# Router logits from the residual stream: the norm's scale folded into the router, the token's root and the shift put on the sums, scale and shift on the gathered rows after their turn

## The chip, the cores and the metric

The kernel runs on one core of a Trainium2 chip. The metric is the device time of one execution in microseconds (us). TensorE (PE) multiplies, VectorE (DVE) and ScalarE (ACT) do elementwise work, GpSimd (POOL) issues the gathers, SyncE (SP) issues the other transfers; each engine runs its instructions strictly in order and waits on semaphores for the others.

## The reference, cut to what matters

The model has two layers. The second ends in a mixture of experts: the stream `x` (512 tokens of 1024 numbers) is normed and modulated, a router picks two of eight experts per token, and each expert is a SwiGLU of 3584 hidden numbers over the tokens that chose it.

```python
h = rmsnorm(x, norm2_g) * (1 + sc2) + sh2      # x * root * A + B, root per token, A and B per column
logits = h @ router                            # 1024 x 8
top_logit, top_idx = lax.top_k(logits, 2)
gates = softmax(top_logit)
y = (silu(h[tok] @ w1[e]) * (h[tok] @ w3[e])) @ w2[e] * gate
out = x + g2 * scatter_add(y)
```

The kernel keeps fp32 accuracy by splitting each operand of a product into a high and a low part (fp32r), and multiplying the parts.

## The kernel before, in words

The stages follow each other: a first norm, the RG-LRU mixer, a dense SwiGLU, attention, `route`, `moe`, `final`. Up to `route` the stream lies turned in SBUF: `xT`, partitions are columns of the model (8 blocks of 128, `k`), the free axis is tokens.

`attention` leaves its last output projections to `route`: `self.attn_outs(cs, segs)` does, for column blocks `cs` and a range of tokens, 24 matmuls per block (8 `k` times three products of parts, L155, L157, L159) and adds the result to `xT` (L384). `route` takes the tokens in two halves of 256. It projects blocks 4 to 7 of the first half, then calls `norm` for it (squares L361, their sum L363, root L335 and L336, the root spread over the partitions by PE L344, times scale L372, plus shift L377, split L166 and L167) with block 4 of the second half put between. `norm` writes `h2` (fp32, turned) and the parts for the logits. Blocks 5 to 7 of the second half follow, then its norm; while that runs, the first half's logits are made (L983). `rows` turns 128 tokens back to rows (8 transposes, L973), copies them from PSUM (L975) and writes them to DRAM: `xd` holds the stream's rows, to which the experts later add, and `h2d` the normed rows, from which the experts gather. After the second half's logits come top-2, the counts, the ranks of the experts by load and the places of the tokens (L1023 to L1080), all small DVE work.

`moe` takes the experts in four pairs, a big and a small one. `gather` makes the token indices (L1174 to L1194) and fetches rows of `h2d` by an indirect DMA on POOL (L1190). The weights come as 1 MB tiles `raw` on SP's queue (L1155), four buffers deep; the first needs the expert's number, `eidi` (L1421), in an SP register. Each `raw` is split in two halves: `hi` by ACT (L166), `lo` by DVE (L167). `gathered` turns the gathered rows (L1231, into PSUM pool `tr`, two buffers) and splits them into `XG`, the parts that the expert's first matmuls read; one ACT and one DVE instruction serve four column blocks. `hidden` (128 tokens; L1262 to L1264) and `hidden_t` (more tokens; L1286 to L1289) are woven; so are `outputs` and `outputs_t`. Within the output stage of a pair the next pair is gathered and turned.

The program text is not the order on the engines: a list scheduler orders each engine's instructions when the kernel is built, by dependencies and its own costs.

Of the kernel before, what the change touches and what calls it, by code (L numbers as in the profile page):

```python
# [10 lines left out]
F32 = mybir.dt.float32  # L11
F32R = mybir.dt.float32r
# [3 lines left out]
AF = mybir.ActivationFunctionType  # L16
ALU = mybir.AluOpType
# [68 lines left out]
class Net:  # L86
# [859 lines left out]

    def route(self):

        nc, I, tc = self.nc, self.I, self.tc
        V, S, mm = nc.vector, nc.scalar, nc.tensor.matmul  # L950
        LAT = SEGS[:1]
# [6 lines left out]
        with ExitStack() as st:  # L958
            one = self.pool(st, "rt1", 1)
            two = self.pool(st, "rt2", 2)  # L960
            rraw = one.tile([P, KT, 8], F32, name="rraw")
            nc.gpsimd.dma_start(rraw, I["moe_router"][0].rearrange("(k p) e -> p k e", p=P))
            rt = one.tile([P, KT, 16], F32R, name="rt")
            V.tensor_copy(rt[:, :, 0:8], rraw)
            V.tensor_tensor(rt[:, :, 8:16], rraw, rt[:, :, 0:8].bitcast(F32), op=ALU.subtract)
            h2 = one.tile([P, KT, L], F32, name="h2")
            lg = one.tile([P, 4, 8], F32, name="lg")

            def rows(src, dst, j):

                ps = self.ptile("prow")
                for k in range(KT):
                    nc.tensor.transpose(ps[:, k * P:(k + 1) * P], src[:, k, j * P:(j + 1) * P], self.ident)  # L973
                ht = two.tile([P, D], F32, tag="ht", name="ht", bufs=3)
                S.activation(ht, ps, AF.Copy)  # L975
                nc.sync.dma_start(dst[j * P:(j + 1) * P, :], ht)

            def logits(parts, i):

                pl = self.sp.tile([P, 512], F32, tag="sm", name="plog")  # L980
                for k in range(KT):
                    for x in parts:
                        mm(pl[0:16, 0:C], rt[:, k], x[:, k], start=(k == 0 and x is parts[0]), stop=(k == KT - 1 and x is parts[1]))  # L983
                lrow = two.tile([16, C], F32, tag="lrow", name="lrow")
                V.tensor_copy(lrow, pl[0:16, 0:C])
                pt = self.sp.tile([P, 512], F32, tag="sm", name="plt")
                for j in range(2):
                    nc.tensor.transpose(pt[:, 16 * j:16 * j + 16], lrow[:, j * P:(j + 1) * P], self.ident[:16, :16])
                pv = pt[:, 0:32].rearrange("p (j e) -> p j e", j=2)
                d = lg[:, 2 * i:2 * i + 2]  # L990
                V.tensor_copy(d, pv[:, :, 8:16])
                V.tensor_tensor(d, pv[:, :, 0:8], d, op=ALU.add)

            x = self.xT[0]
            parts = [[self.big.tile([P, KT, C], F32R, tag=f"{x}{1 - i}", name=f"n{x}") for x in ("HH", "HL")] for i in range(2)]
            self.attn_outs(range(4, 8), HALVES[:1])
            self.norm(1, 1, HALVES[0], two, out=parts[0], full=h2, between=lambda: self.attn_outs([4], HALVES[1:]))
            for c in (5, 6, 7):  # L1000
                self.attn_outs([c], HALVES[1:])
                if c < 7:
                    rows(x, self.xd, c - 5)

            def beside():
                logits(parts[0], 0)
                rows(x, self.xd, 2)

            self.norm(1, 1, HALVES[1], two, out=parts[1], full=h2, between=beside)
            for j in range(2):  # L1010
                rows(h2, self.h2d, j)
            rows(x, self.xd, 3)
            logits(parts[1], 1)
            for j in (2, 3):
                rows(h2, self.h2d, j)
            self.dumpx("x3")
            self.wst_stack.close()
            self.keep = kp = self.pool(self.ctx, "keep", 1, side="right")
# [204 lines left out]
    def gathered(self, X):  # L1223

        n = X["n"]
        XG = X["XG"] = self.mo1.tile([P, KT, 2 * n], F32R, tag=f"XG{X['slot']}", name="XG")
        for gx, a, m in X["gxs"]:
            for k0 in (0, 4):
                pt = self.tr.tile([P, 512], F32, tag="tr", name="pgx")
                for k in range(4):  # L1230
                    self.nc.tensor.transpose(pt[:, k * m:(k + 1) * m], gx[:m, (k0 + k) * P:(k0 + k + 1) * P], self.ident[:m, :m])  # L1231
                pv = pt[:, :4 * m].rearrange("p (k t) -> p k t", k=4)
                self.split(XG[:, k0:k0 + 4, a:a + m], XG[:, k0:k0 + 4, n + a:n + a + m], pv)
            yield

    def flush(self):
# [13 lines left out]
    def hidden_512(self, X, ch):  # L1250
        nc = self.nc
        V, S, mm = nc.vector, nc.scalar, nc.tensor.matmul
        xh, xl = X["XG"][:, :, 0:P], X["XG"][:, :, P:2 * P]
        both = self.psum()
# [43 lines left out]
    def hidden_t(self, X):  # L1298
# [247 lines left out]
```

## Time and profile before

| | |
|---|---|
| median of 3 runs | 2392.67 us (2392.31 to 2395.7) |
| profiled execution | 2390.89 us, of which the span from first to last instruction 2389.1 us |
| TensorE's mean granted clock | 0.988 of full speed |
| PE busy | 2310.9 us (97%) |
| DVE, ACT busy | 1731.5 us (72%), 1326.3 us (56%) |
| `route` and the start of `moe` | about 1075 to 1170 us of the span |

The page's line of engine busy time over 40 slices shows PE at 9 tenths or more nearly everywhere; the first slice and the twentieth (about 1135 to 1195 us) have 7 tenths, the last 5. The change lies in and just before that twentieth slice. Times in a timeline are counted from the start of the span.

### The profile page before, as it was taken

How to read it: one execution, taken by the hardware profiler on the slowest of the kernel's cores; microseconds unless marked ns; L12 is line 12 of the kernel's file. 1: busy time of each engine (PE TensorE's matmuls, PEld its weight loads, DVE VectorE, ACT ScalarE, POOL GpSimd, SP SyncE). 2: the span in 40 equal slices, each digit the busy share in tenths (PEclk: the TensorE clock that was granted, in tenths of full speed). 3: DMA queues.
4: the chain of work that ended last, by engine and by line, in shares of the span. 5: the costliest groups of instructions: out<-in, count | busy, mean ns of one | idle time of the engine just before them, and what ended most of it. 6: DMA issues, size and time to landing. Idle time of an engine off the chain costs nothing. (4 is left out here: it accounts for less than half of the span.)

```text
span 2389.1 us, 37939 instructions
## 1 busy us (share of the span) xinstructions
PE 2310.9 (97%) x14911; PEld 2064.7 (86%) x14911; DVE 1731.5 (72%) x2610; ACT 1326.3 (56%) x1882; POOL 44.4 (2%) x40
## 2 busy tenths in 40 slices
PE   7999999999999999999799999999999999999995
PEld 6887888888888888898699999999999999999994
DVE  7668776555564366795888877888778887788874
ACT  5687342112211146774566665767667776677763
POOL 0000000000000000000100000000010000100000
PEclk9999999999999999999799999999999999999997
DMA  9255423243431112001888889999899998999995
GB/s 306 80 168 193 160 71 124 84 145 124 141 124 53 54 45 71 19 2 57 298 286 286 293 279 287 319 302 310 290 309 314 300 311 289 311 322 307 307 314 170
DMA packets 349434, 491.18 MB, mean 206 GB/s; under 512 B 8848, under 2 KB 247696, under 8 KB 349248
## 3 DMA queue, kind: packets, MB, share of 16 engines
q1 hardware_dynamic: 346032, 477.50, 60.3%
q0 software_dynamic: 3216, 11.18, 2.0%
q8 instruction: 119, 1.95, 0.3%
q14 instruction: 67, 0.55, 0.1%
HBM read 477.04 MB, written 11.60 MB: 205 GB/s over the span
## 5 line engine op out<-in xcount | busy, mean ns | idle before, releaser
L167 DVE TENSOR_TENSOR lo<-raw,hi 128x1024 fp32r<-128x1024 f32 (+2 forms) x856 | 930.4, 1107 | 250.5 <-ACT hi L166 245.3
L166 ACT ACTIVATE hi<-raw 128x1024 fp32r<-128x1024 f32 (+2 forms) x856 | 803.8, 964 | 474.2 <-PE hb L1289 228.4
L1289 PE MATMUL hb<-XG,hi 128*128 128x320 f32 (+2 forms) x1568 | 428.8, 348 | 0.0
L1287 PE MATMUL hb<-XG,lo 128*128 128x160 f32 (+2 forms) x1792 | 398.6, 242 | 0.0
L1287 PEld LDWEIGHTS hb<-XG,lo 128*128 128x128 f32 x1792 | 332.1, 190 | 4.4
L1289 PEld LDWEIGHTS hb<-XG,hi 128*128 128x128 f32 x1568 | 295.1, 188 | 0.0
L1289 PE MATMUL hb<-HT,hi 128*128 128x320 f32 (+2 forms) x864 | 231.4, 348 | 0.0
L1287 PE MATMUL hb<-HT,lo 128*128 128x160 f32 (+2 forms) x896 | 211.1, 239 | 0.0
L157 PE MATMUL p<-HL,hi 128*128 128x512 f32 (+1 forms) x704 | 191.3, 338 | 0.0
L159 PE MATMUL p<-HH,lo 128*128 128x512 f32 (+1 forms) x704 | 191.1, 337 | 0.0
L155 PE MATMUL p<-HH,hi 128*128 128x512 f32 (+1 forms) x704 | 191.1, 338 | 0.0
L1262 PE MATMUL hb<-hi,XG 128*128 128x512 f32 x448 | 177.9, 397 | 1.6 <-ACT XG L166 1.6
L1263 PE MATMUL hb<-hi,XG 128*128 128x512 f32 x448 | 177.3, 396 | 0.0
L1264 PE MATMUL hb<-lo,XG 128*128 128x512 f32 x448 | 176.8, 395 | 0.0
L1287 PEld LDWEIGHTS hb<-HT,lo 128*128 128x128 f32 x896 | 169.9, 190 | 2.3
L1289 PEld LDWEIGHTS hb<-HT,hi 128*128 128x128 f32 x864 | 162.2, 188 | 1.6
L653 DVE TENSOR_TENSOR sg<-p,sg 128x768 f32<-128x768 f32 (+2 forms) x26 | 21.7, 835 | 151.3 <-PE p L159 151.3
L1294 ACT ACTIVATE t<-hb 128x320 f32<-128x320 f32 (+2 forms) x128 | 56.9, 445 | 126.2 <-PE hb L1289 126.2
L157 PEld LDWEIGHTS p<-HL,hi 128*128 128x128 f32 x704 | 112.9, 189 | 15.2
L155 PEld LDWEIGHTS p<-HH,hi 128*128 128x128 f32 x704 | 112.8, 189 | 15.3
L159 PEld LDWEIGHTS p<-HH,lo 128*128 128x128 f32 x704 | 112.7, 189 | 15.3
L384 DVE SCALAR_TENSOR_TENSOR xT<-py,acol,xT 128x512 f32<-128x512 f32 (+1 forms) x176 | 101.5, 611 | 22.4 <-PE py L159 21.9
(410 smaller groups left out, 4070.0 us busy)
## 6 DMA issues: line engine op xcount, KB each, us to landing
raw<-in_moe_w_dram SPq DMA_DIRECT2D x280, 1024.0 KB, 5.2
raw<-in_moe_w_dram SPq DMA_DIRECT2D x64, 896.0 KB, 4.9
raw<-in_ffn_w_dram SPq DMA_DIRECT2D x33, 1024.0 KB, 5.2
raw<-in_ada_w_dram SPq DMA_DIRECT2D x24, 1024.0 KB, 7.0
araw<-in_ada_w_dram SPq DMA_DIRECT2D x48, 512.0 KB, 3.7
raw<-in_rg_w_in_dram SPq DMA_DIRECT2D x16, 512.0 KB, 6.6
raw<-in_attn_w_qkv_dram SPq DMA_DIRECT2D x6, 1024.0 KB, 5.0
raw<-in_rg_w_out_dram SPq DMA_DIRECT2D x4, 1024.0 KB, 8.1
```

The costliest lines, as they stand in the source:

```text
L155: mm(ps[:, s:e], wh, xh[v][:, s - v * L:e - v * L], start=(first and i == 0), stop=False)
L157: mm(ps[:, s:e], wh, xl[v][:, s - v * L:e - v * L], start=False, stop=False)
L159: mm(ps[:, s:e], wl, xh[v][:, s - v * L:e - v * L], start=False, stop=(last and i == n - 1))
L166: self.nc.scalar.activation(hi, src, AF.Copy)
L167: self.nc.vector.tensor_tensor(lo, src, hi.bitcast(F32), op=ALU.subtract)
L384: self.nc.vector.scalar_tensor_tensor(x, ps[:, s:e], gate[:, k, v:v + 1], x, op0=ALU.mult, op1=ALU.add)
L1262: mm(ps, xh[:, kk], hi[:, k], start=(kk == 0), stop=False)
L1263: mm(ps, xl[:, kk], hi[:, k], start=False, stop=False)
L1264: mm(ps, xh[:, kk], lo[:, k], start=False, stop=(kk == 7))
L1287: mm(ps[:, 0:n], wl, x[:, 0:n], start=False, stop=False)
L1289: mm(ps[:, 0:2 * n], wh, x, start=False, stop=last)
L1294: self.nc.scalar.activation(t, ps[:, :, n:2 * n], AF.Copy)
```

## The change

Before, the normed stream was computed in full for all 512 tokens, used for the logits, turned to rows and written to `h2d`. Now three factors are taken apart. With A the column scale, B the column shift and r the token's root, the logits are r * (x @ (A * router)) + B @ router. So the router is multiplied by A once (`ra`), `B @ router` is made once (`pb`, `br`), the split parts are those of `x` itself (`split_x`), and `finish` puts r and `br` on the eight sums of a token. The root no longer goes over the partitions; it stays a column, one number per token row. `rows` turns `x` once and copies it twice, once times r for `h2d` and once as it is for `xd`. The rows gathered from `h2d` thus lack A and B; `gathered` puts them on after the turn, where columns are partitions: per column block, one ACT instruction for the high part and one DVE instruction for the fp32 value `z`, then one subtraction for the low part of four blocks.

```diff
+            A, B = self.A[1][:, 1], self.mod(1, 3)
+            ra = one.tile([P, KT, 8], F32, name="ra")
+            V.tensor_tensor(ra, rraw, A[:, :, 0:1].to_broadcast((P, KT, 8)), op=ALU.mult)
...
+            for k in range(KT):
+                mm(pb[:, 0:8], B[:, k, 0:1].to_broadcast((P, P)), rraw[:, k], start=(k == 0), stop=(k == KT - 1))
...
+            def split_x(i, *ks):
+                s, e, _ = HALVES[i]
+                for k in ks:
+                    self.split(parts[i][0][:, k], parts[i][1][:, k], x[:, k, s:e])
...
+            def rows(js, r):
...
+                for dst in (self.h2d, self.xd):
+                    for j, ps in zip(js, pss):
+                        ht = two.tile([P, D], F32, tag="ht", name="ht", bufs=3)
+                        S.activation(ht, ps, AF.Copy, scale=r[:, j % 2:j % 2 + 1] if dst is self.h2d else 1.0)
+                        nc.sync.dma_start(dst[j * P:(j + 1) * P, :], ht)
...
-            self.attn_outs(range(4, 8), HALVES[:1])
-            self.norm(1, 1, HALVES[0], two, out=parts[0], full=h2, between=lambda: self.attn_outs([4], HALVES[1:]))
...
-            self.norm(1, 1, HALVES[1], two, out=parts[1], full=h2, between=beside)
-            for j in range(2):
-                rows(h2, self.h2d, j)
-            rows(x, self.xd, 3)
-            logits(parts[1], 1)
-            for j in (2, 3):
-                rows(h2, self.h2d, j)
+            def finish(i, r):
+                for j in range(2):
+                    d = lg[:, 2 * i + j]
+                    V.scalar_tensor_tensor(d, d, r[:, j:j + 1], br, op0=ALU.mult, op1=ALU.add)
...
+            r0 = inverse(0)
+            logits(0)
+            finish(0, r0)
             for c in (5, 6, 7):
                 self.attn_outs([c], HALVES[1:])
+                split_x(1, c)
                 if c < 7:
-                    rows(x, self.xd, c - 5)
+                    rows((c - 5,), r0)
+            logits(1)
+            r1 = inverse(1)
+            finish(1, r1)
+            rows((2, 3), r1)
...
     def gathered(self, X):
...
-                pv = pt[:, :4 * m].rearrange("p (k t) -> p k t", k=4)
-                self.split(XG[:, k0:k0 + 4, a:a + m], XG[:, k0:k0 + 4, n + a:n + a + m], pv)
+                z = self.mo2.tile([P, 512], F32, tag="sg", name="z")
+                for k in range(4):
+                    c = slice(k * m, (k + 1) * m)
+                    sc, b = A[:, k0 + k, 0:1], B[:, k0 + k, 0:1]
+                    S.activation(XG[:, k0 + k, a:a + m], pt[:, c], AF.Identity, bias=b, scale=sc)
+                    self.nc.vector.tensor_scalar(z[:, c], pt[:, c], sc, b, op0=ALU.mult, op1=ALU.add)
+                zv = z[:, :4 * m].rearrange("p (k t) -> p k t", k=4)
+                hi = XG[:, k0:k0 + 4, a:a + m].bitcast(F32)
+                self.nc.vector.tensor_tensor(XG[:, k0:k0 + 4, n + a:n + a + m], zv, hi, op=ALU.subtract)
```

`inverse(i)` is what `norm` did up to the root: squares on ACT, their sum on DVE, one PE product and the root.

The order on VectorE around the second half's logits, before (`h2` is the normed stream, `nHH` and `nHL` its parts, `lrow` the logits out of PSUM, `lg` the logits turned):

```order
L372 SCALAR_TENSOR_TENSOR h2_9734<-xT0_2118,A1_95,rs_10125 128x256
L167 TENSOR_TENSOR nHL_9739<-h2_9734,nHH_9738 128x256 x2
L1023 MAX mx_10248<-lg_9735 128x8 x2
L1024 MAX_INDEX mi_10249<-mx_10248,lg_9735 128x8 x2
L167 TENSOR_TENSOR nHL_9739<-h2_9734,nHH_9738 128x256 x3
L985 COPY lrow_10213<-plog_10196 16x256
L991 COPY lg_9735<-plt_10215 128x16
L992 TENSOR_TENSOR lg_9735<-plt_10215,lg_9735 128x16
L1023 MAX mx_10248<-lg_9735 128x8 x2
```

and of the changed kernel, from the last addition to the stream (`po1`) on (`xHH`, `xHL` are the parts of the stream, `rcol` the root):

```order
L384 SCALAR_TENSOR_TENSOR xT0_2118<-po1_10073,acol1_93,xT0_2118 128x256
L1118 CAST iota_10255<-ct_75 128x192
L1120 CAST tokid_10257<-ct_75 128x12
L1157 MEMSET cum_10410 128x1
L167 TENSOR_TENSOR xHL_9751<-xT0_2118,xHH_9750 128x256
L994 TENSOR_TENSOR acc_10125<-acc_10125,sq_10145 128x256
L1016 COPY lrow_10118<-plog_10101 16x256
L1022 COPY lg_9747<-plt_10120 128x16
L1023 TENSOR_TENSOR lg_9747<-plt_10120,lg_9747 128x16
L336 RECIPROCAL rcol_10151<-rcol_10151 128x2
L1028 SCALAR_TENSOR_TENSOR lg_9747<-lg_9747,rcol_10151,br_9745 128x8 x2
L1058 MAX mx_10190<-lg_9747 128x8 x2
```

Between the last addition and the logits there is now one split; the eight multiplications by scale and root are gone.

The order on ScalarE at the start of `moe`, before (`XG_10525` is the input of the small expert, the one whose matmuls stand first on PE, `XG_10510` that of the big one; `hi_10561` and `hi_10565` are halves of the first weight tile, `hi_10585` begins the second):

```order
L1150 ACTIVATE g2b_10491<-hb_10492 128x1024
L166 ACTIVATE hi_10561<-raw_10559 128x1024
L166 ACTIVATE XG_10525<-pgx_10526 128x4x128
L166 ACTIVATE XG_10525<-pgx_10533 128x4x128
L166 ACTIVATE hi_10565<-raw_10559 128x1024
L166 ACTIVATE hi_10585<-raw_10583 128x1024
```

and of the changed kernel (`XG_10483` is the small expert's input; `hi_10551`, `hi_10555` are of the first weight tile, `hi_10575`, `hi_10579` of the second, `hi_10621` of the third):

```order
L166 ACTIVATE hi_10555<-raw_10549 128x1024
L1272 ACTIVATE XG_10452<-pgx_10468,acol1_93,A1_95 128x128
L1185 ACTIVATE g2b_10433<-hb_10434 128x1024
L1272 ACTIVATE XG_10483<-pgx_10484,acol1_93,A1_95 128x128
L166 ACTIVATE hi_10575<-raw_10573 128x1024
L166 ACTIVATE hi_10579<-raw_10573 128x1024
L1272 ACTIVATE XG_10452<-pgx_10468,acol1_93,A1_95 128x128
L1272 ACTIVATE XG_10483<-pgx_10484,acol1_93,A1_95 128x128
L166 ACTIVATE hi_10621<-raw_10619 128x1024
L1272 ACTIVATE XG_10483<-pgx_10499,acol1_93,A1_95 128x128
L1272 ACTIVATE XG_10483<-pgx_10484,acol1_93,A1_95 128x128
```

The small expert's input now stands behind the splits of three weight tiles, where it stood behind one half of the first.

The order on VectorE there, before (`lo` belongs to `hi`; `room` is a scratch table):

```order
L167 TENSOR_TENSOR lo_10562<-raw_10559,hi_10561 128x1024
L1140 TENSOR_TENSOR room_10457<-eid_10301,room_10457 128x128
L167 TENSOR_TENSOR XG_10525<-pgx_10526,XG_10525 128x4x128
L1141 TENSOR_REDUCE room_10457<-room_10457 128x16
L167 TENSOR_TENSOR XG_10525<-pgx_10533,XG_10525 128x4x128
```

and of the changed kernel the end of the same stretch, which begins at `lo_10552`, 26 instructions ahead of the last row here:

```order
L1273 TENSOR_SCALAR z_10504<-pgx_10499,A1_95,acol1_93 128x128
L1176 TENSOR_REDUCE room_10399<-room_10399 128x16
L1273 TENSOR_SCALAR z_10489<-pgx_10484,A1_95,acol1_93 128x128
L1273 TENSOR_SCALAR z_10504<-pgx_10499,A1_95,acol1_93 128x128
L167 TENSOR_TENSOR lo_10576<-raw_10573,hi_10575 128x1024
L1273 TENSOR_SCALAR z_10489<-pgx_10484,A1_95,acol1_93 128x128
L1273 TENSOR_SCALAR z_10504<-pgx_10499,A1_95,acol1_93 128x128
L1276 TENSOR_TENSOR XG_10483<-z_10489,XG_10483 128x4x128
```

Its first low part, on which the second matmul of the small expert waits, moved from the second place behind the first `lo` to the twenty-sixth.

## Rows read from the trace of the kernel before

**Rows 1.** Busy time by engine in stretches; behind PEclk DMA share, GB/s.
```profile
core 0: us, PE busy (x) PEld busy (x) DVE busy (x) ACT busy (x) POOL busy (x), PEclk, DMA share, GB/s
1130.00:1140.00 10.00, 4.68 (x33) 3.11 (x32) 7.05 (x44) 8.10 (x15) 0.95 (x1) 0.93 0.50 202
1140.00:1150.00 10.00, 4.09 (x31) 3.63 (x32) 8.77 (x71) 0.00 (x0) 4.56 (x5) 0.50 0.33 106
1150.00:1160.00 10.00, 5.82 (x28) 4.92 (x26) 5.75 (x24) 4.25 (x7) 0.00 (x0) 0.67 1.02 348
1160.00:1170.00 10.00, 9.21 (x43) 7.28 (x43) 8.22 (x12) 7.01 (x9) 0.53 (x1) 0.70 0.97 332
1170.00:1200.00 30.00, 30.00 (x186) 28.12 (x185) 27.00 (x43) 22.09 (x28) 0.00 (x0) 1.00 0.94 313
```

**Rows 2.** The same by stretches of 40 us: first and last of the experts.
```profile
1200.00:1240.00 40.00, 40.00 (x243) 37.23 (x242) 32.50 (x35) 27.59 (x36) 0.00 (x0) 1.00 0.89 292
...
2280.00:2320.00 40.00, 40.00 (x266) 36.63 (x265) 31.17 (x32) 25.57 (x28) 0.00 (x0) 1.00 0.94 313
```

**Rows 3.** Timeline of PE: start, us, instruction, count, idle before and releaser.
```profile
1107.57 0.61 PE L333 MATMUL rsum<-ones,acc 128*128 128x1 f32 x4
...
1120.80 0.28 PE L159 MATMUL po<-HH,lo 128*128 128x256 f32 x1
...
1123.10 0.28 PE L983 MATMUL plog<-nHH,rt 128*16 128x256 f32 x1
...
1124.96 0.38 PE L344 MATMUL rs<-ct,rcol 128*128 128x128 f32 x2
...
1159.57 0.79 PE L1262 MATMUL hb<-hi,XG 128*128 128x512 f32 x1 [1.64 <-ACT XG L166]
...
1161.76 0.79 PE L1263 MATMUL hb<-hi,XG 128*128 128x512 f32 x1
```

**Rows 4.** Timeline of VectorE, from the norm to the expert number.
```profile
1125.50 0.46 DVE L372 SCALAR_TENSOR_TENSOR h<-xT,A,rs 128x256 f32<-128x256 f32 x1
...
1135.99 0.24 DVE L1023 MAX8 mx<-lg 128x8 f32<-128x8 f32 x2
...
1141.57 1.13 DVE L1174 TENSOR_SCALAR sel<-iota,posr 128x192 bf16<-128x192 bf16 x6
...
1145.29 0.14 DVE L1421 SCALAR_TENSOR_TENSOR eidi<-idf,eid 1x8 int32<-1x8 f32 x1
```

**Rows 5.** Timeline of SyncE's queue at the first weight tiles.
```profile
1147.12 26.45 SPq L1155 DMA_DIRECT2D raw<-in_moe_w_dram  x8
```

**Rows 6.** Timeline of ScalarE at the first three weight tiles.
```profile
1157.97 1.06 ACT L166 ACTIVATE hi<-raw 128x1024 fp32r<-128x1024 f32 x1 [3.42 <-DMA raw<-in_moe_w_dram]
...
1162.64 1.06 ACT L166 ACTIVATE hi<-raw 128x1024 fp32r<-128x1024 f32 x1 [1.69 <-DMA raw<-in_moe_w_dram]
...
1165.36 2.01 ACT L166 ACTIVATE hi<-raw 128x1024 fp32r<-128x1024 f32 x2 [0.17 <-DMA raw<-in_moe_w_dram]
```

**Rows 7.** Durations (ns min/median/max, first and last start) of instructions like the new ones.
```profile
L166 ACT ACTIVATE XG<-pgx x24: 223/582/598, 1150.9 to 2009.7; 128x512 fp32r<-128x512 f32 x16, 128x128 fp32r<-128x128 f32 x4, 128x256 fp32r<-128x256 f32 x2, 128x64 fp32r<-128x64 f32 x2
L167 DVE TENSOR_TENSOR XG<-pgx,XG x24: 215/681/685, 1153.1 to 2011.1; 128x512 fp32r<-128x512 f32 x16, 128x128 fp32r<-128x128 f32 x4, 128x256 fp32r<-128x256 f32 x2, 128x64 fp32r<-128x64 f32 x2
...
L377 ACT ACTIVATE h<-h,acol x16: 492/494/512, 1111.2 to 1132.2; 128x256 f32<-128x256 f32 x16
...
L1148 DVE TENSOR_SCALAR room<-ct,acol x8: 270/286/514, 1146.8 to 1152.7; 128x128 f32<-128x128 f32 x8
...
L246 DVE TENSOR_SCALAR zT<-zT,A,acol x16: 404/469/547, 25.0 to 47.9; 128x512 f32<-128x512 f32 x8, 128x256 f32<-128x256 f32 x8
```

**Rows 8.** Timeline of VectorE, low parts of weights back to back.
```profile
1165.56 5.76 DVE L167 TENSOR_TENSOR lo<-raw,hi 128x1024 fp32r<-128x1024 f32 x5
```

**Rows 9.** Timeline of PE in the first output stage, the next pair's turns.
```profile
1392.57 1.03 PE L1231 MATMUL pgx<-ct,gx 128*128 128x128 f32 x8
...
1400.25 0.68 PE L1231 MATMUL pgx<-ct,gx 32*128 32x32 f32 x8
```

More of the change, by code (lines that the diff above doesn't have):

```diff
@@ L962, in route @@
             nc.gpsimd.dma_start(rraw, I["moe_router"][0].rearrange("(k p) e -> p k e", p=P))
+            A, B = self.A[1][:, 1], self.mod(1, 3)
+            ra = one.tile([P, KT, 8], F32, name="ra")
+            V.tensor_tensor(ra, rraw, A[:, :, 0:1].to_broadcast((P, KT, 8)), op=ALU.mult)
             rt = one.tile([P, KT, 16], F32R, name="rt")
-            V.tensor_copy(rt[:, :, 0:8], rraw)
-            V.tensor_tensor(rt[:, :, 8:16], rraw, rt[:, :, 0:8].bitcast(F32), op=ALU.subtract)
-            h2 = one.tile([P, KT, L], F32, name="h2")
@@ L967, in route @@
-            lg = one.tile([P, 4, 8], F32, name="lg")
-            def rows(src, dst, j):
-                ps = self.ptile("prow")
-                for k in range(KT):
[L973 to L978, printed above, removed]
+            V.tensor_copy(rt[:, :, 0:8], ra)
@@ new lines, in route @@
+            V.tensor_tensor(rt[:, :, 8:16], ra, rt[:, :, 0:8].bitcast(F32), op=ALU.subtract)
+            pb = self.sp.tile([P, 512], F32, tag="sm", name="pb")
+            for k in range(KT):
+                mm(pb[:, 0:8], B[:, k, 0:1].to_broadcast((P, P)), rraw[:, k], start=(k == 0), stop=(k == KT - 1))
+            br = one.tile([P, 8], F32, name="br")
+            V.tensor_copy(br, pb[:, 0:8])
+            lg = one.tile([P, 4, 8], F32, name="lg")
+            x = self.xT[0]
+            parts = [[one.tile([P, KT, C], F32R, tag=f"{t}{i}", name=f"x{t}") for t in ("HH", "HL")] for i in range(2)]
@@ new lines, in split_x, with inverse @@
+            def split_x(i, *ks):
+                s, e, _ = HALVES[i]
+                for k in ks:
+                    self.split(parts[i][0][:, k], parts[i][1][:, k], x[:, k, s:e])
+            def inverse(i):
+                s, e, _ = HALVES[i]
+                acc = two.tile([P, C], F32, tag="acc", name="acc")
+                for k in range(KT):
+                    sq = two.tile([P, C], F32, tag="sq", name="sq") if k else acc
+                    S.activation(sq, x[:, k, s:e], AF.Square)
+                    if k:
+                        V.tensor_tensor(acc, acc, sq, op=ALU.add)
+                return self.inv_rms_cols(acc, C, D, two)
@@ new lines, in rows @@
+            def rows(js, r):
+                pss = [self.ptile("prow") for _ in js]
+                for j, ps in zip(js, pss):
+                    for k in range(KT):
+                        nc.tensor.transpose(ps[:, k * P:(k + 1) * P], x[:, k, j * P:(j + 1) * P], self.ident)
+                for dst in (self.h2d, self.xd):
+                    for j, ps in zip(js, pss):
+                        ht = two.tile([P, D], F32, tag="ht", name="ht", bufs=3)
+                        S.activation(ht, ps, AF.Copy, scale=r[:, j % 2:j % 2 + 1] if dst is self.h2d else 1.0)
+                        nc.sync.dma_start(dst[j * P:(j + 1) * P, :], ht)
@@ L980, in logits @@
+            def logits(i):
                 pl = self.sp.tile([P, 512], F32, tag="sm", name="plog")
                 for k in range(KT):
-                    for x in parts:
-                        mm(pl[0:16, 0:C], rt[:, k], x[:, k], start=(k == 0 and x is parts[0]), stop=(k == KT - 1 and x is parts[1]))
+                    for p in range(2):
+                        mm(pl[0:16, 0:C], rt[:, k], parts[i][p][:, k], start=(k == 0 and p == 0), stop=(k == KT - 1 and p == 1))
                 lrow = two.tile([16, C], F32, tag="lrow", name="lrow")
@@ L992, in logits @@
                 V.tensor_tensor(d, pv[:, :, 0:8], d, op=ALU.add)
-            x = self.xT[0]
-            parts = [[self.big.tile([P, KT, C], F32R, tag=f"{x}{1 - i}", name=f"n{x}") for x in ("HH", "HL")] for i in range(2)]
-            self.attn_outs(range(4, 8), HALVES[:1])
-            self.norm(1, 1, HALVES[0], two, out=parts[0], full=h2, between=lambda: self.attn_outs([4], HALVES[1:]))
+            def finish(i, r):
+                for j in range(2):
+                    d = lg[:, 2 * i + j]
+                    V.scalar_tensor_tensor(d, d, r[:, j:j + 1], br, op0=ALU.mult, op1=ALU.add)
+            split_x(0, *range(4))
+            for c in range(4, 8):
+                self.attn_outs([c], HALVES[:1])
+                split_x(0, c)
+            split_x(1, *range(4))
+            self.attn_outs([4], HALVES[1:])
+            split_x(1, 4)
+            r0 = inverse(0)
+            logits(0)
+            finish(0, r0)
             for c in (5, 6, 7):
                 self.attn_outs([c], HALVES[1:])
+                split_x(1, c)
                 if c < 7:
-                    rows(x, self.xd, c - 5)
-            def beside():
-                logits(parts[0], 0)
-                rows(x, self.xd, 2)
-            self.norm(1, 1, HALVES[1], two, out=parts[1], full=h2, between=beside)
-            for j in range(2):
-                rows(h2, self.h2d, j)
-            rows(x, self.xd, 3)
-            logits(parts[1], 1)
-            for j in (2, 3):
-                rows(h2, self.h2d, j)
+                    rows((c - 5,), r0)
[3 more added lines that the diff above has]
+            rows((2, 3), r1)
             self.dumpx("x3")
@@ L1225, in gathered @@
         n = X["n"]
+        S, A, B = self.nc.scalar, self.A[1][:, 1], self.mod(1, 3)
         XG = X["XG"] = self.mo1.tile([P, KT, 2 * n], F32R, tag=f"XG{X['slot']}", name="XG")
```

## The prediction

> **What bounds the kernel now.** I read the stretches by engine first, then the timelines of PE, VectorE and ScalarE across the hole that they show. In the experts PE is the bound: all 28 stretches of 40 us from 1200 to 2320 hold 40.00 us of PE at clock 1.00 [rows 2]. So a microsecond by which the experts' stream of matmuls starts earlier comes off the end, and one by which PE is held up inside it is added. The only hole near the change is 1130 to 1170: PE 4.68, 4.09, 5.82 and 9.21 of 10 us, and the clock falls to 0.50, the 1.2 GHz level, after PE has gone idle [rows 1]. From 1170 on PE is full again.
>
> What fills the hole is a chain: the last projection ends (last matmul 1120.80), the second half is normed (first scaling 1125.50), split, its logits made and turned, MAX8 at 1135.99, places at 1141.57, the expert's number at 1145.29, the first weight DMA at 1147.12, the first split of a landed weight tile at 1157.97 [rows 3 to 6]. The reader is to see that ScalarE waited 3.42 us for that tile. The first expert matmul starts at 1159.57, the second, which reads the low part of the input, at 1161.76, and PE is busy from there. So there are two parts: how much earlier the weights are called, and how long after their landing the second matmul runs.
>
> **The route, part by part.** Earlier in the projections PE gets three additions. The product `pb` is 8 fp32 products; `rsum` shows that two such take four records in 0.61 us, with the tail of the last in it [rows 3], so 0.12 to 0.15 a record and 1.9 to 2.4 us for 16; I take 1.9, since more PE work follows. The first half's logits (1123.10 to 1124.96, 1.86 us) and their turn (0.3 with a short wait) now stand ahead of block 5 instead of behind block 7. Gone from there are a wait of 0.65 for the root and 0.2 for spreading it. The last projection's matmul thus starts 1.9 + 1.86 + 0.3 - 0.85 = 3.2 us later, at 1124.0. PE is the busy one there, so the new splits (a pass of 0.42 each on ACT and DVE) hide under the 2.9 us that each block takes.
>
> From that matmul to MAX8 it took 15.2 us. What is left of it: the matmul's end 0.3, the addition 0.5, a high part 0.45, a low part 0.45, the last logits matmul 0.35, out of PSUM 0.45, turn 0.35, two `lg` steps 0.4, then the root's tail. The product `rsum` stands behind the turn on PE (0.5); root 0.3, reciprocal 0.2, the two `finish` steps 0.3, together 0.9 more than the `lg` steps cover. The sum is about 4.4, so MAX8 comes at 1128.4, 7.6 earlier. Five transposes of rows stand ahead of the turn but run beside the copy out of PSUM. The order now puts the gate's arithmetic behind the places and behind the number, about 0.9 us. The tanh it needs stands behind three row copies and a table load on ScalarE and ends by my count half a microsecond before it is asked for. So the number is ready 8.5 earlier, and with it the first weight DMA (about 1138.6). The last rows written by SP stand ahead of it in that queue, but are out of ACT at about 1133. The weight tiles land as long after their issue as before, since the same gathers run beside them: first split at 1157.97 - 8.5 = 1149.5.
>
> **The gathered rows, part by part.** Here the change adds: per four column blocks 4 ACT and 5 DVE instructions in place of 1 and 1. None of them is in the trace. A scaled ACT pass on 128 numbers lies between 0.22 (the 64-wide copy, the least of the group) and 0.49 (256 wide with a column operand); I take 0.37, or 0.3 from start to start, as passes overlap by a little [rows 7]. For `z` on DVE the nearest is the 128-wide product with a column, 0.29, which starts every 0.2; the other end is the 256-wide one with two columns, 0.40. I take 0.25 from start to start, with 0.2 and 0.33 as bounds. A subtraction of 512 numbers is 0.68, every 0.6 [rows 7].
>
> Before, the second matmul came 3.8 us after the first weight tile's split began (1161.76 - 1157.97). Now count VectorE from the end of that first high part, 1.05 after: three low parts at 1.15 (five take 5.76 [rows 8]) 3.45, two subtractions for the big expert and one for the small 1.8, nine `z` 2.25, table steps of `room` and `cum` 1.75. That is 9.25, and the matmul runs 10.3 us after the tile. ScalarE gives the same: the third tile lands 7.4 after the first (1165.36 - 1157.97 [rows 6]), its high part 0.96, then four passes that the small expert's first blocks need, 1.2, and the subtraction with its handover 0.7: 10.3. So 10.3 - 3.8 = 6.5 of the 8.5 us are given back, and the second matmul runs at about 1159.8. That is 2.0 earlier; with `z` at its bounds 2.4 or 1.2. Behind it PE has work: the next weight tiles are called when low parts are done, which is still earlier than before.
>
> ScalarE's copies of 512 take 0.58 and the 256-wide pass with one column 0.49 [rows 7]. The Trainium skill (ScalarE: Activation LUTs, What ACT_TABLE_LOAD costs) has a rule for this that speaks against cutting passes into four: 186 ns plus 0.833 ns per element, 93 ns more for each column operand, with neighbours overlapping by 93. The trace agrees (the rule makes 0.61 and 0.49). It would make the new pass 0.48 and the step from start to start 0.39, an estimate from that page; ScalarE's count would then be 10.7 and the gain 1.6 in place of 2.0.
>
> **Later pairs.** In the three later gathers the new passes lie beside a full PE, with VectorE at 31 to 33 of 40 us [rows 2], and cost nothing unless PE has to wait for a PSUM buffer of the turns. There are two; both are taken by the first turns at 1392.57 and wanted again at 1400.25, 6.7 us after those end [rows 9]. ScalarE's eight passes with three weight splits between them need about 2.4 + 2.9, so that fits. The next user is the turned output, some 4.9 us behind the second turns by the matmuls between; there the passes, held by a split that waits for PE, end at about the same moment. I put 0 to 0.5 us a pair, 0.7 in all.
>
> **Sum.** -8.5 + 6.5 + 0.7 = -1.3 us. The profiled execution took 2390.89 (span 2389.1), 1.8 under the median of 2392.67; the sum goes onto the median: 2391.4.
>
> **The rivals.**
> (1) The experts keep all of the earlier start: the input's passes find gaps, because weights land later or earlier than I count, and PE starts as soon after the tile as before. For it: VectorE was idle for much of 1150 to 1160 (5.75 busy [rows 1]). Against it: the orders are fixed, and three splits stand ahead. With most or all of the 8.5: 2384 to 2387.
> (2) Slower: the turns hold their two PSUM buffers too long in the later pairs. PE stops in front of each next user, three places in each of three pairs, at its full rate, so nothing hides it. It decides as soon as eight passes and the splits between them last longer than the 6.7 or 4.9 us above; at 0.8 us a place this is 7 us, less the 2.0 gained: 2397.7. For it: every pass waits its turn behind splits that wait for PE. Against it: before, PE never waited there, and by my count one place in three is tight.
> (3) The clock: PE now idles from about 1128 to 1159 with a few turns between, longer than before. If the half rate lasts 2 us longer behind the restart, that costs 1 us; the rest as forecast: 2392.4.
> (4) The change does not move the weights' call: the last logits still wait for something I took as hidden (the root, the rows' copies on ScalarE). Each pass of 1.0 ahead of the root would cost 1. Gain gone: 2392 to 2395.
>
> **How the numbers follow.** No change means within 0.2%, 4.8 us, about what a measurement of this kernel can tell. The forecast has 0.50 (its own range 2389.5 to 2393), (3) 0.12, (4) 0.13, all within 0.2%: 0.75. (1) has 0.13, counted as faster; (2) 0.12, counted as slower. The range from 2385.5 to 2397 leaves out the ends of (1) and (2), some 0.15 to 0.2.
>
> **What would show it.** In the changed profile: the last projection's matmul at about 1124, MAX8 at 1128.4, the first weight DMA at 1138.6, the first split of a tile at 1149.5, the second expert matmul about 10 us behind that and not 4. MAX8 later than 1131 would break the route's count. A second matmul within 6 us of the tile would make it (1); waits of PE for `tr` buffers in the output stages, with stretches under 40.00, would make it (2).

## The result, and the profile after

The changed kernel takes 2406.78 us (median, 2405.64 to 2407.85) against 2392.49 of the kernel before (2391.42 to 2395.70): ratio 1.0054, 95% interval 1.0043 to 1.0066. So it is 14.3 us, 0.5%, slower. Forecast were 2391.4, with 2397.0 as the upper end of the range; the median lies 9.8 above that end. A second set of runs gave 2407.15 and 1.0063 (1.0046 to 1.0080). The profiled execution took 2405.64, its span 2403.9.

I read the two traces by four landmarks that both have: the last wide matmul of the output projections (W, just ahead of the first instruction that the change adds), the first weight DMA of the experts (D), the first turn of hidden columns (H, the small expert's; TensorE runs full from there on), the last turn of outputs (E). The timeline of TensorE before has W, H and E:

```profile
1094.13 0.39 PE L159 MATMUL po<-HH,lo 128*128 128x512 f32 x1
...
1193.17 0.60 PE L1277 MATMUL pht<-ct,sg 128*128 128x128 f32 x4
...
2361.71 0.39 PE L1370 MATMUL pyt<-ct,t 128*16 128x128 f32 x2 [0.58 <-DVE yt L1371]
```

and after, with the steps between them (beside [rows 3]):

```profile
1098.62 0.39 PE L159 MATMUL po<-HH,lo 128*128 128x512 f32 x1
1098.84 1.85 PE L974 MATMUL pb<-rraw,acol 128*128 128x8 f32 x16
...
1127.94 0.28 PE L159 MATMUL po<-HH,lo 128*128 128x256 f32 x1
...
1157.43 0.79 PE L1305 MATMUL hb<-hi,XG 128*128 128x512 f32 x1 [0.99 <-ACT XG L1272]
...
1160.50 1.12 PE L1267 MATMUL pgx<-ct,gx 128*128 128x128 f32 x4 [2.27 <-DVE z L1273]
...
1165.01 0.68 PE L1267 MATMUL pgx<-ct,gx 64*128 64x64 f32 x4 [3.39 <-DVE z L1273]
...
1165.92 0.79 PE L1306 MATMUL hb<-hi,XG 128*128 128x512 f32 x1 [0.23 <-DVE XG L1276]
...
1197.93 0.60 PE L1320 MATMUL pht<-ct,sg 128*128 128x128 f32 x4
...
2377.09 0.39 PE L1413 MATMUL pyt<-ct,t 128*16 128x128 f32 x2 [0.58 <-DVE yt L1414]
```

VectorE, SyncE's queue and ScalarE after, beside [rows 4], [rows 5] and [rows 6]:

```profile
1132.25 0.29 DVE L1058 MAX8 mx<-lg 128x8 f32<-128x8 f32 x2
...
1141.28 0.14 DVE L1464 SCALAR_TENSOR_TENSOR eidi<-idf,eid 1x8 int32<-1x8 f32 x1
```
```profile
1143.29 9.80 SPq L1190 DMA_DIRECT2D raw<-in_moe_w_dram  x4
```
```profile
1153.42 1.06 ACT L166 ACTIVATE hi<-raw 128x1024 fp32r<-128x1024 f32 x1 [3.03 <-DMA raw<-in_moe_w_dram]
```

So W to D went from 52.99 (1147.12 - 1094.13) to 44.67, 8.3 won. D to H went from 46.05 to 54.64, 8.6 lost. H to E went from 1168.54 to 1179.16, 10.6 lost. The other 4.5 are in W itself: lost ahead of the change, where TensorE's order is the same in both kernels.

The stretches by engine show the same two losses (beside [rows 1] and [rows 2]; the second block is from before, the others from after):

```profile
1140.00:1150.00 10.00, 3.77 (x25) 3.12 (x26) 8.92 (x50) 1.78 (x5) 5.37 (x6) 0.50 0.70 228
1150.00:1160.00 10.00, 5.95 (x20) 4.00 (x19) 8.06 (x31) 6.85 (x11) 0.00 (x0) 0.50 1.02 358
1160.00:1170.00 10.00, 5.88 (x20) 4.16 (x21) 9.35 (x24) 6.72 (x15) 0.54 (x1) 0.50 0.51 176
```
```profile
1400.00:1440.00 40.00, 40.00 (x245) 36.44 (x244) 29.40 (x33) 25.08 (x29) 0.00 (x0) 1.00 0.82 279
1680.00:1720.00 40.00, 40.00 (x263) 36.77 (x262) 30.78 (x34) 26.04 (x31) 0.00 (x0) 1.00 0.82 280
2000.00:2040.00 40.00, 40.00 (x261) 36.57 (x260) 30.93 (x34) 25.53 (x30) 0.00 (x0) 1.00 0.88 296
```
```profile
1200.00:1240.00 40.00, 40.00 (x246) 37.43 (x244) 33.44 (x36) 27.84 (x37) 0.00 (x0) 1.00 0.87 287
1400.00:1440.00 40.00, 38.04 (x234) 34.40 (x232) 34.53 (x56) 28.73 (x46) 0.00 (x0) 1.00 0.76 253
1680.00:1720.00 40.00, 37.59 (x236) 34.05 (x234) 32.54 (x46) 27.28 (x41) 0.00 (x0) 0.96 0.81 265
...
2000.00:2040.00 40.00, 37.24 (x239) 33.57 (x238) 35.17 (x55) 29.00 (x47) 0.00 (x0) 1.00 0.75 249
```

From 1160 to 1170 TensorE has 5.88 of 10 us where it had 9.21, still at 0.50, the 1.2 GHz level. The three stretches in which the next pair's rows are turned were 40.00 and are 38.04, 37.59 and 37.24: 7.1 us of the 10.6. In the second of them TensorE's clock is also 0.96 instead of 1.00. After the wait that ends at 1712.08 it is granted 0.50, the 1.2 GHz level, for a short while (0.50 from 1713 to 1716), and 0.04 of 40 us is another 1.6. The last 1.9 I have not split. Who holds TensorE there is said by its waits, in the first and the second of these pairs:

```profile
1412.71 0.44 PE L1413 MATMUL pyt<-ct,t 128*128 128x128 f32 x2 [1.75 <-DVE z L1273]
...
1710.03 0.43 PE L1267 MATMUL pgx<-ct,gx 32*128 32x32 f32 x4
...
1712.08 0.43 PE L1267 MATMUL pgx<-ct,gx 32*128 32x32 f32 x4 [1.62 <-DVE z L1273]
...
1720.00 0.44 PE L1413 MATMUL pyt<-ct,t 128*128 128x128 f32 x2 [0.65 <-DVE z L1273]
```

All three that wait are the next users of a `tr` buffer. The new passes, with what the two engines waited for (beside [rows 7]), and the timelines of ScalarE and VectorE in the first of these pairs:

```profile
L1273 DVE TENSOR_SCALAR z<-pgx,A,acol x96: 285/404/413, 1147.6 to 2032.5; 128x128 f32<-128x128 f32 x64, 128x32 f32<-128x32 f32 x16, 128x64 f32<-128x64 f32 x8, 128x16 f32<-128x16 f32 x8
...
  ACT XG L1272: 5.1, 12
```
```profile
L1272 ACT ACTIVATE XG<-pgx,acol,A x96: 344/446/462, 1147.1 to 2031.2; 128x128 fp32r<-128x128 f32 x64, 128x32 fp32r<-128x32 f32 x16, 128x64 fp32r<-128x64 f32 x8, 128x16 fp32r<-128x16 f32 x8
...
  DVE z L1273: 8.2, 11
```
```profile
1400.58 0.79 ACT L1272 ACTIVATE XG<-pgx,acol,A 128x128 fp32r<-128x128 f32 x2
1401.26 0.95 ACT L166 ACTIVATE hi<-raw 128x896 fp32r<-128x896 f32 x1
1402.29 0.81 ACT L1272 ACTIVATE XG<-pgx,acol,A 128x128 fp32r<-128x128 f32 x2
1403.93 0.81 ACT L1272 ACTIVATE XG<-pgx,acol,A 128x128 fp32r<-128x128 f32 x2 [0.83 <-DVE z L1273]
```
```profile
1401.85 0.72 DVE L1273 TENSOR_SCALAR z<-pgx,A,acol 128x128 f32<-128x128 f32 x2
1402.49 1.08 DVE L167 TENSOR_TENSOR lo<-raw,hi 128x896 fp32r<-128x896 f32 x1
1403.49 0.72 DVE L1273 TENSOR_SCALAR z<-pgx,A,acol 128x128 f32<-128x128 f32 x2
1404.42 0.76 DVE L1273 TENSOR_SCALAR z<-pgx,A,acol 128x128 f32<-128x128 f32 x2 [0.21 <-ACT XG L1272]
```

The two engines go in step: one column block of each of the two buffers on ScalarE, then the same on VectorE, each round with a weight split in between, 1.6 to 2.0 us a round. ScalarE waits for `z` and VectorE for ScalarE's pass, though neither reads what the other has written: they wait for the buffer that both read. The Trainium skill has that as a rule (PSUM — Partial Sum Buffer, PSUM bank collisions raise a hardware error): the compiler back end's scheduler adds a dependency between any two instructions on different engines that touch the same bank and group of 32 partitions, two reads included. The trace agrees (8.2 and 5.1 us of such waits, start and later pairs together).

### The profile page after: what moved, and what is told of

Same layout as the page of the kernel before. It is cut to its first block, busy times and chain, and to the rows that moved or that the text cites. A ratio compares the mean times of both kernels' runs of the same rounds, so it can differ in the third digit from the quotient of the medians.

```text
span 2403.9 us, 38040 instructions
## 1 busy us (share of the span) xinstructions
PE 2316.8 (96%) x14891; PEld 2069.1 (86%) x14891; DVE 1756.4 (73%) x2696; ACT 1340.8 (56%) x1938; POOL 43.2 (2%) x40
```

## The experiments

Theory A: the route wins what was forecast and the passes over the turned rows lose it; A1 says by the alternation of the two engines on one buffer, A2 by the amount of work. The table has all runs: W, the three distances, the median, and the ratio to the runs of before beside it.

| kernel | W | W to D | D to H | H to E | median | ratio (95%) |
|---|---|---|---|---|---|---|
| before | 1094.13 | 52.99 | 46.05 | 1168.54 | 2392.49 | |
| e11 before again | 1094.67 | 52.94 | 45.81 | 1168.60 | 2390.05 (one run) | |
| changed | 1098.62 | 44.67 | 54.64 | 1179.16 | 2406.78 | 1.0054 (1.0043 to 1.0066) |
| e10 changed again | 1094.37 | 44.77 | 56.27 | 1180.84 | 2407.15 | 1.0063 (1.0046 to 1.0080) |
| e1 route only | 1096.18 | 44.80 | 46.54 | 1168.56 | 2383.09 | 0.9956 (0.9939 to 0.9972) |
| e2 passes only | 1096.93 | 52.93 | 57.36 | 1180.71 | 2416.28 | 1.0103 (1.0085 to 1.0120) |
| e3 VectorE alone | 1096.68 | 44.78 | 55.78 | 1170.04 | 2395.47 | 1.0007 (0.9998 to 1.0017) |
| e4 ScalarE alone | 1095.77 | 44.76 | 48.84 | 1170.43 | 2388.43 | 0.9989 (0.9979 to 0.9998) |
| e4 again | 1094.78 | 44.67 | 49.17 | 1170.42 | 2389.68 | 0.9984 (0.9976 to 0.9993) |
| e5 two loops | 1094.16 | 44.79 | 55.77 | 1170.52 | 2396.13 | 1.0013 (1.0004 to 1.0022) |
| e6 rows scaled | 1101.70 | 50.76 | 43.91 | 1168.66 | 2395.34 | 1.0009 (1.0000 to 1.0018) |
| e7 e4, shift summed | 1094.76 | 43.14 | 48.73 | 1170.42 | 2388.60 | 0.9983 (0.9974 to 0.9991) |
| e8 rows on VectorE | 1105.77 | 48.09 | 43.28 | 1168.66 | 2392.00 | 0.9995 (0.9986 to 1.0004) |
| e9 rows, no column write | 1094.23 | 46.20 | 42.19 | 1168.61 | 2381.65 | 0.9956 (0.9943 to 0.9969) |

**Half the change each.** e1 puts the old split back:

```diff
-    S.activation(XG[:, k0 + k, a:a + m], pt[:, c], AF.Identity, bias=b, scale=sc)
-    self.nc.vector.tensor_scalar(z[:, c], pt[:, c], sc, b, op0=ALU.mult, op1=ALU.add)
...
+    self.split(XG[:, k0:k0 + 4, a:a + m], XG[:, k0:k0 + 4, n + a:n + a + m], pv)
```

> The changed route, with the turns of the gathered rows as they were before (no scale and no shift on the experts' input, which is left out of what is computed). Theory A (the loss lies in the passes over the turned rows): the first weight DMA keeps what the changed route won. In the changed kernel it came 3.8 us earlier although the stretch ahead of the change ran 4.5 us later, so 8.3 us by itself; the second expert matmul is again about 4 us behind the first split of a tile, no stretch of the later pairs is under 40.00, and the time is 2392.5 - 8.3 = 2384 (2382 to 2386). Theory B (half of the loss comes from the 4.5 us by which everything ahead of the change is late, whatever the passes do): 2388 to 2390. Theory C (clock): the half rate lasts past 1165 as in the changed kernel and eats 2 us, 2386 to 2388.

It leaves scale and shift out of what is computed, so it is no version to use. 2383.09: theory A. W to D keeps 8.2, D to H is within 0.5 of before, H to E the same. e2 is the kernel before with the new `gathered`:

> The route of before, with the changed passes over the turned rows (scale and shift are thus put on twice). Theory A: second expert matmul some 12 us behind the first split instead of 3.8, and 3 to 3.5 us lost in each of the three later pairs: 2392.5 + 8.5 + 10 = 2411 (2408 to 2413). Theory B: 2400 to 2403, as the passes then account for only some 8 to 10 us. If the route is what costs: 2392 to 2396.

2416.28, 24.0 slower (its table row: 0, 11.3 and 12.2), more than I expected (2408 to 2413) but nothing of it in the route. The halves add up: -9.2 and +24.0 make 14.8 against 14.3 measured.

**Which part of the passes.** e3 and e4 leave the buffer to one engine:

```diff
     for k in range(4):
...
-        S.activation(XG[:, k0 + k, a:a + m], pt[:, c], AF.Identity, bias=b, scale=sc)
         self.nc.vector.tensor_scalar(z[:, c], pt[:, c], sc, b, op0=ALU.mult, op1=ALU.add)  # e3 keeps this line
+        S.activation(z[:, c], pt[:, c], AF.Identity, bias=b, scale=sc)                     # e4 has this one in its place
...
+    self.split(XG[:, k0:k0 + 4, a:a + m], XG[:, k0:k0 + 4, n + a:n + a + m], zv)
```

> The changed kernel, but VectorE alone reads the turned rows: four scaled passes into z as now, then one ScalarE copy of 512 from z for the high part and the subtraction. VectorE's instructions are those of the changed kernel; ScalarE has one for four. Theory A1 (two engines that read one PSUM buffer by turns, each pass waiting for the other engine's, hold the buffer): the wait of TensorE for z goes from 10 us to 2 or less, 2 to 3 us come back in each later pair and 1 to 3 at the start: 2406.8 - 9 = 2398 (2395 to 2400). Theory A2 (the passes' own time on VectorE, which is as long as before): 2405 to 2408.

> The same with ScalarE as the only reader: four scaled passes of ScalarE into z, one ScalarE copy of 512 for the high part, one subtraction on VectorE. ScalarE has 0.58 us more a buffer than in the changed kernel, VectorE 1.5 us less. Theory A1: nothing alternates, so later pairs get 2 to 3 us back each; at the start VectorE loses nine z (3.5 us), the second matmul comes 8 to 10 us behind the tile: 2394 to 2398. Theory A2 with ScalarE as the holder: 2405 to 2410; with VectorE as the holder: 2395 to 2399, as A1, so this run tells A1 from A2 only together with the one before.

In the later pairs A1 holds: H to E falls from 1179.16 to 1170.04 and 1170.43. At the start A2 does: with `z` on VectorE D to H stays at 55.78, with it on ScalarE it is 48.84. In e3 the second matmul itself came sooner, 9.35 us behind the first split of a tile instead of 12.5, but H did not: from that matmul to H it took 35.94 us instead of 32.01, as TensorE waited for VectorE again a few matmuls later. Order moves the second matmul; how much VectorE has to do sets H. For e4 I expected 2394 to 2398; it is 2388.43, since moving `z` off VectorE gives back 7 at the start and not 3.5. Run again, it gave 2389.68 and 0.9984: the time 0.7 above what I expected, the ratio as expected, so it was not luck:

> The version in which ScalarE alone reads the turned rows, once more in five rounds: 2388 to 2389, ratio to before 0.998 to 0.9995. If it was luck, 2391 to 2393.

e5 keeps both readers and every instruction, and writes two loops in place of one, so that a buffer changes hands once:

```diff
     for k in range(4):
...
         S.activation(XG[:, k0 + k, a:a + m], pt[:, c], AF.Identity, bias=b, scale=sc)
+    for k in range(4):
...
         self.nc.vector.tensor_scalar(z[:, c], pt[:, c], sc, b, op0=ALU.mult, op1=ALU.add)
```

> The changed kernel with its nine passes a buffer in another program order: first ScalarE's four, then VectorE's four (two loops in place of one). Instructions, shapes and amounts of work on both engines are those of the changed kernel; what changes is that a buffer passes between the engines once and not seven times. Theory A1 (the alternation holds the buffers in the later pairs, VectorE's own time costs at the start): the later pairs' 10 us fall to 2 or 3, as with VectorE alone; the start stays within 2 us of the changed kernel's, as VectorE has the same work: 2397 to 2400. Theory A2 (the amount of work everywhere): 2405 to 2408. If the alternation is also what costs at the start: 2389 to 2393.

2396.13, 0.9 under its range, with H to E 1170.52 and D to H 55.77. Its three stretches:

```profile
1400.00:1440.00 40.00, 39.83 (x245) 36.08 (x244) 34.70 (x52) 27.35 (x42) 0.00 (x0) 1.00 0.79 273
1680.00:1720.00 40.00, 39.61 (x261) 36.15 (x259) 35.16 (x56) 30.44 (x50) 0.00 (x0) 1.00 0.79 266
2000.00:2040.00 40.00, 39.63 (x259) 35.97 (x258) 36.23 (x57) 29.08 (x44) 0.00 (x0) 1.00 0.80 275
```

This run decides between A1 and A2 in the later pairs, as the work is the same to the instruction: TensorE is nearly full beside a VectorE as busy as in the changed kernel, and its clock stays at 1.00. The alternating order cost 8.6 to 10.3 us there (against the first and the second profile of the changed kernel). What the run does not part is the handovers from the weight splits between them: with two loops the scheduler also puts ScalarE's eight passes in one row (2.88 us from 1395.34 on) and the splits behind it. At the start H came no sooner, though the second matmul did (8.84 us behind the tile).

**The stretch ahead of the change.** Both kernels once more, unchanged:

> The changed kernel itself once more. By the runs so far its loss is -8.3 (route), +8.6 (start of the experts) and +10.6 (later pairs) = 10.9, but 14.3 were measured; in its profile 4.5 us were lost ahead of the first instruction that the change adds, where the order on TensorE is the same. Theory F (that part varies from execution to execution): the last wide output matmul, at 1098.62 there, comes at 1094 to 1097, with the rest as before, and the time is 2403 to 2406. Rival (it belongs to this kernel): again 1098 to 1099, and 2406 to 2408.

> The kernel before once more, for how much the stretch ahead of the change varies by itself. Theory F: its last wide output matmul, at 1094.13 there, at 1093 to 1098. Rival (it doesn't vary): within 0.5 of 1094.1.

Theory F for W: 1094.37 instead of 1098.62, so those 4.5 us belonged to the one profiled execution (in the ten of the table whose order on TensorE is alike up to there, from before to e5, W runs from 1094.13 to 1098.62). What sets W in each is open, and e11, at 1094.67, decides nothing. But the time of the changed kernel did not fall with W (2407.15, not 2403 to 2406): in this execution the two losses are 10.2 and 12.3, and -8.2 + 10.2 + 12.3 = 14.3, where the profiled executions of e10 and e11 lie 14.8 apart. Of the 1.6 more at the start, 1.1 is the first tile, whose split began 11.21 us behind its call (1150.35 - 1139.14) instead of 10.13, and 0.6 lies behind the second matmul. The 1.7 more in the later pairs is TensorE's clock. In e10 it is below 1.00 in two of the three stretches, where in the first profile it was in one:

```profile
1400.00:1440.00 40.00, 38.04 (x225) 34.55 (x224) 33.07 (x53) 26.63 (x42) 0.00 (x0) 0.96 0.74 247
1680.00:1720.00 40.00, 37.60 (x234) 33.89 (x232) 32.52 (x47) 27.28 (x41) 0.00 (x0) 0.96 0.80 270
```

TensorE's busy time in the three is the same in both profiles to 0.01 us; the second 0.96 is worth 1.6.

**Versions that may beat both.** e7 is e4 with another product for the shift:

```diff
-for k in range(KT):
-    mm(pb[:, 0:8], B[:, k, 0:1].to_broadcast((P, P)), rraw[:, k], ...)
+V.tensor_tensor(rb, rraw, B[:, :, 0:1].to_broadcast((P, KT, 8)), op=ALU.mult)
+for k in range(1, KT):
+    V.tensor_tensor(rb[:, 0], rb[:, 0], rb[:, k], op=ALU.add)
+mm(pb[:, 0:8], self.ones, rb[:, 0], start=True, stop=True)
```

> As the run beside it, but the shift's product with the router made otherwise: VectorE multiplies and adds the eight blocks, and one fp32 product with ones takes the place of TensorE's eight (1.85 us in the changed kernel's trace). Theory A (TensorE sets the pace ahead of the last projection, so pb's 1.85 count in full): 1.5 less than the run beside it, 2386.5 to 2387.5, and the last residual comes 1.5 us sooner behind the first product of the output projections. Rival (the residuals or splits set the pace there): no difference.

W to D is 1.5 shorter in the trace (43.14 against 44.67). The median, 2388.60, missed its range; it is 1.1 under that of e4 again, but the intervals of the two ratios overlap, so the time does not show the gain. e6 puts scale and shift on ahead of the rows' write:

```diff
+V.tensor_scalar(y[:, k, s:e], x[:, k, s:e], A[:, k, 0:1], None, op0=ALU.mult)   # turned for h2d
...
+nc.gpsimd.dma_start(bd.rearrange("(k p) o -> p k o", p=P), B[:, :, 0:1])         # then read back as a row
...
+nc.gpsimd.tensor_tensor(ht, ht, brow, op=ALU.add)
```

> Scale and shift put on ahead of the rows' write, as a version that may beat all: VectorE multiplies each split block by the norm scale while the projections run, these are turned, ScalarE puts the root on, GpSimd adds the shift as a row (fetched by a small DMA), and the gathered rows are split as before. The rows of the stream itself are written behind the last logits. Theory A: nothing stands between turn and matmul, so this is the route alone: 2383 to 2386. Rival (the rows now come later, through GpSimd's addition, and the gather waits for them; or the row copies, eight behind the last logits, hold the SP queue ahead of the weights): each us of that counts fully up to the first weight tile, 2386 to 2391.

2395.34, above both ranges. The later pairs and D to H are as good as hoped, but W is 1101.70 and W to D 50.76. VectorE's timeline there, and in e8, where VectorE adds the row itself:

```profile
1136.76 2.25 DVE L1082 TENSOR_TENSOR M<-E,E 128x32 f32<-128x32 f32 x1
1139.05 3.15 DVE L1085 CAST Mb<-M 128x32 bf16<-128x32 f32 x1
1141.23 1.59 DVE L1089 TENSOR_TENSOR Mp<-Mp,M 128x8 f32<-128x8 f32 x4
```
```profile
1143.09 0.19 DVE L1083 TENSOR_TENSOR M<-E,E 128x32 f32<-128x32 f32 x1
1143.32 0.18 DVE L1086 CAST Mb<-M 128x32 bf16<-128x32 f32 x1
1143.41 0.77 DVE L1090 TENSOR_TENSOR Mp<-Mp,M 128x8 f32<-128x8 f32 x4
```

```diff
-S.activation(ht, ps, AF.Copy, scale=1.0 if r is None else r[:, j % 2:j % 2 + 1])
...
-nc.gpsimd.tensor_tensor(ht, ht, brow, op=ALU.add)
+V.scalar_tensor_tensor(ht, ps, r[:, j % 2:j % 2 + 1], brow, op0=ALU.mult, op1=ALU.add)
```

> As the version with scaled rows, but root and shift are put on by one VectorE instruction out of PSUM; GpSimd adds nothing. In that version's trace three small VectorE instructions behind MAX8 (M, Mb, Mp) took 2.25, 3.15 and 1.59 us while GpSimd added the shift, against 0.19, 0.18 and 0.76 in the run of the route alone. Theory D (GpSimd's pass slows VectorE): they are back at about 0.2, 0.2 and 0.8, which gives 5.9 back, less two row passes of about 1.2 on VectorE if they stand ahead of the gate: 2389 to 2392. Rival (they were late for another reason, such as TensorE or the row copies): still over 1 us each, and the time within 1 us of 2395.

Theory D, and 2392.00. What is left is W, late in both: near 620 TensorE waited 5.7 us (e6's trace), as VectorE waited for modulation weights, and behind that wait its clock fell too (0.66 from 620 to 630, in the kernel before 1.00). In e8 a further 3.7 us were lost ahead of that, at the write's issue (610.16 against 606.44). e9 writes the shift as whole rows and takes e7's product:

```diff
-nc.gpsimd.dma_start(bd.rearrange("(k p) o -> p k o", p=P), B[:, :, 0:1])
...
+nc.tensor.transpose(pt[:KT, 0:P], B[:, :, 0], self.ident)
...
+V.tensor_copy(bs, pt[:KT, 0:P])
...
+nc.gpsimd.dma_start(bd, bs)
```

> The rows version with VectorE's root and shift once more, with two edits: the shift is turned on TensorE and written to DRAM as 8 rows of 512 bytes (in the two runs before as 1024 single numbers, issued at 606 us, where VectorE then waited 6.64 us for modulation weights and TensorE 5.7), and the shift's product with the router is summed on VectorE. Theory E (the write of single numbers held up the weights' transfer): no wait of TensorE near 620, 7 us back, and 1.5 for the product: 2392.0 - 8.5 = 2383.5 (2382 to 2386), the fastest version with the whole computation. Rival (the wait near 620 has another cause, such as the pool's new size): still there, 2390 to 2391.

W is back at 1094.23 and the time is 2381.65, a little under its range and 0.4% under before: the fastest with the whole computation in it, and level with e1, which leaves a part out (both 0.9956). Its D to H is 4.4 us shorter even than that of e1: 2.2 of it is the first tile, split 8.94 us behind its call instead of 11.10, 1.4 the second matmul (1.45 us behind the tile instead of 2.89), 0.8 lies behind it. Why the tile came sooner is open.

## Why the prediction was wrong, step by step

- **The route** was right. The last projection matmul stands 29.3 us behind W (before 26.7): 2.65 later, forecast 3.2, with `pb` 1.85 for 1.9. From there to MAX8 it is 4.3 for 4.4 (the terms that I had listed add up to 4.15). W to D is 8.3 shorter for 8.5. The marks that I had named (1128.4, 1138.6) were missed by 3.9 and 4.7 because W was 4.5 late; in e10 they are 1128.01 and 1139.14.
- **The start of the experts** was right in kind, too small in size. The second matmul ran 12.5 us behind the tile (1165.92 - 1153.42; 12.49 in the second profile), not 10.3, so 8.7 were given back and not 6.5. VectorE sets this, as counted: with `z` off it, in e4, the matmul runs 5.5 behind. Of the 2.2, 0.75 is `z`: the nine take 3.00 us, mostly 0.32 from start to start, where I took 0.25. I had taken the nearest row, a pass out of SBUF, where the far end, 0.33, was right. Another 0.8 is that the first low part begins at 1155.25 and not with the end of its high part at 1154.48. A `z` stands ahead of it that had waited 1.60 us for ScalarE's pass, and I had not counted it. Another 0.6 is the table steps, 2.33 us for 1.75, with a wait of 0.19 for ScalarE's pass in them. The last 0.1 is the subtractions.
- **The later pairs are the step that failed**: "ScalarE's eight passes with three weight splits between them need about 2.4 + 2.9, so that fits", and 0.7 us for all three. The durations in it are not far off (four passes take 1.50 in a row in the trace of e4). What is wrong is that the passes do not run by themselves: each waits for VectorE's pass on the same buffer, and that stands behind a weight's low part. The eight passes took 6.6 us in the first pair (1398.55 to 1405.18), which just fitted, and 8.3 in the second (1703.70 to 1712.03), where I had 5.3. The next eight held the turned output of the first pair for 1.75 us, where I had put 0 to 0.5. 10.6 to 12.3 us came in place of 0.7: 7.1 of waits, 1.6 or 3.2 of a clock that fell behind such waits, 1.9 not split. e5 takes 8.6 to 10.3 of them away by the order alone. The waits between the passes stood in the instruction order; I counted work where I should have counted handovers. I had also leaned on a VectorE busy for 31 to 33 of 40 us, read off the first and last stretch; in the three that matter it had 29.4 to 30.9, and it is not the busy share that held the buffers.
- **Rival (2)** was that mechanism, at 7 us and with a chance of 0.12. The waits alone are those 7 us; the clock in the later pairs stood in no rival. "By my count one place in three is tight" rested on the same count. Rival (1) is refuted by the second matmul, 12.5 us behind the tile. Rival (4) is refuted by W to D. Rival (3): matmuls of 0.63 us, the half rate's, last to about 1170 instead of 1166, but that goes with the late second matmul. From there to H it took 32.0 us (32.6 in e10) against 31.4, so 0.6 to 1.2 at most is the clock's.

The passes on ScalarE have 0.446 at the median, and 0.35 from start to start in a row of four (1.50 in e4). The Trainium skill's rule (ScalarE: Activation LUTs, What ACT_TABLE_LOAD costs) made 0.48 and 0.39 of them, my rows 0.37 and 0.3: the trace lies between.

## What to carry to other kernels

When an instruction that read a PSUM buffer as a whole is cut into column pieces on two engines, count the handovers of the buffer and what stands on each engine between two of them, not the sum of the durations; write the loop so that one engine reads all its pieces before the other begins, or let one engine read alone. Work at the head of a phase is paid on the engine that is already last there (here VectorE), so put it on the other one, or ahead of the data's write. Compare traces by distances between landmarks: the whole span mixed a 4.5 us jitter with three real terms. And count the clock: a wait of 1.6 to 1.8 us inside a full stretch of TensorE cost another 1.6 of clock, in one of three places in one execution and in two of three in another.

## What the runs showed of the hardware that I had not expected

GpSimd's addition of 128x1024 fp32 (two in 4.67 us in e6) stops VectorE: an instruction of 0.19 took 2.25, one of 0.18 took 3.15. The Trainium skill has a rule for the first of the two (SBUF — State Buffer, Who interferes with whom): a VectorE instruction with two SBUF inputs contends with a GpSimd instruction that reads SBUF, by an exclusive lock. The trace agrees: that instruction ends with the first addition (1139.01 and 1138.97), and in e8, without the additions, the same rows have 0.19 and 0.18 again. The second is a CAST with one input, which that sentence does not cover. It ended with the memset that GpSimd had behind its additions (1142.20 and 1142.16). In the changed kernel two CASTs to `val` took 1.73 us, after 0.43 for the two before, and also ended with a GpSimd memset (1145.10 and 1145.06); that I did not test.

A write of 4 KB as 1024 single numbers, on GpSimd's queue, goes with a long wait for weights on SyncE's. In e6 GpSimd issues it at 606.44, and VectorE then has:

```profile
606.44 1.14 POOL L979 DMA_DIRECT2D bd<-acol  x1 [555.38 <-DVE acol L290]
```
```profile
621.62 0.75 DVE L314 SCALAR_TENSOR_TENSOR aacc<-araw,cT,aacc 128x512 f32<-128x512 f32 x1 [6.64 <-DMA araw<-in_ada_w_dram]
```

Before, TensorE has no wait in that stretch. In e9 it has none either; there the write has 8 rows of 512 bytes, and is issued at 1095.96, so the runs don't tell the write's shape from its place.
